# A weighted sum over eight experts: a ring of token slots in place of four load buffers, and three terms of the last tokens on TensorE

## The chip, the cores and the metric

The kernel runs on one core of a Trainium2 chip. The metric is device time in microseconds (us), the median of several executions. The profile and the trace come from one more execution, in which the hardware profiler recorded every instruction and every DMA packet.

## What is computed

For each of 16 x 1024 tokens there are eight expert outputs of 512 numbers and eight weights. The result is the weighted sum over the experts:

```python
batch, seq, n_experts, expert_dim = 16, 1024, 8, 512
weights = combine_weights[..., np.newaxis]
return np.sum(expert_outputs * weights, axis=2).astype(np.float32)
```

Everything is float32. The expert outputs are 268.4 MB, the result 33.6 MB, the weights 0.5 MB. Each expert output is used once, in one multiply and one add.

## The kernel before

The 16,384 tokens are cut into 64 steps of 128 partitions x 2 tokens (J = 2). A token of a partition is one row of 8 x 512 floats, 16 KB; a step's load is 4 MB, 32 KB for each partition, and one stretch of HBM. A "token" below means one such row in each of the 128 partitions, so there are 128 of them; one multiply-add over one expert of one token is a tile of 128 x 512.

Loads (issue_load, L52 to L62) go alternately through SP's and ScalarE's DMA queue, three steps ahead of their use (LA = 3), into four buffers (in_pool). Each step has its own small weight load through GpSimd's queue (L60). The last two steps (K_TAIL = 2) are loaded as two halves each, one token at a time (L59).

For each of the first 62 steps VectorE does all the arithmetic: for each token one multiply by the first weight (L77) and seven multiply-adds into the accumulator in place (L83), one token after the other. The result of a step, 4 KB per partition, is stored through the queue that did not load it (L92).

The last two steps are shared: ScalarE multiplies experts 4 to 7 into bf16 products (L111), VectorE does experts 0 to 3 (L116, L122), adds the products up in two halvings (L130, L135) and onto the accumulator (L138), and each token is stored by itself through SP's queue (L141).

The order on each engine is the order in the program as the tile framework schedules it; a DMA instruction waits in its issuing engine's queue until its buffer is free, and everything behind it on that engine waits too.

Of the kernel before, what the change touches and what calls it, by code (L numbers as in the profile page):

```python
# [1 line left out]

# [4 lines left out]


@with_exitstack  # L10
def kernel(
    ctx: ExitStack,
    tc: tile.TileContext,
    expert_outputs: bass.AP,
    combine_weights: bass.AP,
    out: bass.AP,
):
    nc = tc.nc
    fp32 = mybir.dt.float32
    bf16 = mybir.dt.bfloat16  # L20

    B, S, E, D = expert_outputs.shape
    T = B * S
    P = 128
    J = 2
    n_steps = T // (P * J)

    eo_blk = expert_outputs.rearrange("b s e d -> (b s) e d").rearrange(
        "(n p j) e d -> n p j e d", p=P, j=J
    )  # L30
    w_blk = combine_weights.rearrange("b s e -> (b s) e").rearrange(
        "(n p j) e -> n p j e", p=P, j=J
    )
    o_blk = out.rearrange("b s d -> (b s) d").rearrange(
        "(n p j) d -> n p j d", p=P, j=J
    )

    in_pool = ctx.enter_context(tc.tile_pool(name="in_pool", bufs=4))
    w_pool = ctx.enter_context(tc.tile_pool(name="w_pool", bufs=4))
    out_pool = ctx.enter_context(tc.tile_pool(name="out_pool", bufs=4))  # L40
    prod_pool = ctx.enter_context(tc.tile_pool(name="prod_pool", bufs=2))

    ES = E // 2
    K_TAIL = 2

    load_engines = [nc.sync, nc.scalar]

    LA = 3
    in_tiles: list[bass.AP | None] = [None] * n_steps
    w_tiles: list[bass.AP | None] = [None] * n_steps  # L50

    def issue_load(m: int) -> None:  # L52
        in_t = in_pool.tile([P, J, E, D], fp32, name="in_t")
        w_t = w_pool.tile([P, J, E], fp32, name="w_t")
        if m < n_steps - K_TAIL:
            load_engines[m % 2].dma_start(out=in_t, in_=eo_blk[m])
        else:
            for j in range(J):
                load_engines[m % 2].dma_start(out=in_t[:, j], in_=eo_blk[m, :, j])  # L59
        nc.gpsimd.dma_start(out=w_t, in_=w_blk[m])  # L60
        in_tiles[m] = in_t
        w_tiles[m] = w_t  # L62

    for m in range(min(LA, n_steps)):
        issue_load(m)

    for n in range(n_steps):
        if n + LA < n_steps:
            issue_load(n + LA)
        if n >= n_steps - K_TAIL:  # L70
            continue
        in_tile = in_tiles[n]
        w_tile = w_tiles[n]
        acc = out_pool.tile([P, J, D], fp32)

        for j in range(J):
            nc.vector.tensor_scalar_mul(  # L77
                out=acc[:, j, :],
                in0=in_tile[:, j, 0, :],
                scalar1=w_tile[:, j, 0:1],  # L80
            )
            for e in range(1, E):
                nc.vector.scalar_tensor_tensor(  # L83
                    out=acc[:, j, :],
                    in0=in_tile[:, j, e, :],
                    scalar=w_tile[:, j, e : e + 1],
                    in1=acc[:, j, :],
                    op0=mybir.AluOpType.mult,
                    op1=mybir.AluOpType.add,
                )  # L90

        load_engines[(n + 1) % 2].dma_start(out=o_blk[n], in_=acc)  # L92

    tail_steps = list(range(n_steps - K_TAIL, n_steps))
    tail_accs = {}
    tail_prods = {}
    for n in tail_steps:
        acc = out_pool.tile([P, J, D], fp32, name="acc")
        prods = prod_pool.tile([P, J, E - ES, D], bf16, name="prods")
        tail_accs[n] = acc  # L100
        tail_prods[n] = prods

    for j in range(J):
        for n in tail_steps:
            in_tile = in_tiles[n]
            w_tile = w_tiles[n]
            acc = tail_accs[n]
            prods = tail_prods[n]

            for e in range(ES, E):  # L110
                nc.scalar.mul(  # L111
                    out=prods[:, j, e - ES, :],
                    in_=in_tile[:, j, e, :],
                    mul=w_tile[:, j, e : e + 1],
                )
            nc.vector.tensor_scalar_mul(  # L116
                out=acc[:, j, :],
                in0=in_tile[:, j, 0, :],
                scalar1=w_tile[:, j, 0:1],
            )  # L120
            for e in range(1, ES):
                nc.vector.scalar_tensor_tensor(  # L122
                    out=acc[:, j, :],
                    in0=in_tile[:, j, e, :],
                    scalar=w_tile[:, j, e : e + 1],
                    in1=acc[:, j, :],
                    op0=mybir.AluOpType.mult,
                    op1=mybir.AluOpType.add,
                )
            nc.vector.tensor_add(  # L130
                out=prods[:, j, 0:2, :],
                in0=prods[:, j, 0:2, :],
                in1=prods[:, j, 2:4, :],
            )
            nc.vector.tensor_add(  # L135
                out=prods[:, j, 0, :], in0=prods[:, j, 0, :], in1=prods[:, j, 1, :]
            )
            nc.vector.tensor_add(  # L138
                out=acc[:, j, :], in0=acc[:, j, :], in1=prods[:, j, 0, :]
            )  # L140
            nc.sync.dma_start(out=o_blk[n, :, j], in_=acc[:, j, :])  # L141


# [1 line left out]
_INS = ['expert_outputs', 'combine_weights']  # L145
_OUTS = [((16, 1024, 512), 'float32')]


# [23 lines left out]
```

## Time and profile before

| | |
|---|---|
| median of 5 runs | 721.49 us (721.30 to 721.65) |
| the profiled execution | 721.57 us |
| its span (first to last instruction) | 719.8 us |
| VectorE busy | 644.3 us, 90% |
| ScalarE busy | 11.4 us, 2% |
| DMA moved | 302.63 MB, 420 GB/s over the span |
| busy multiply-adds (L83) | 580.1 us, 868 of 744 ns each |

The profile cuts the span into 40 equal slices of 18 us and gives for each the busy tenths of an engine, and for the DMA engines the busy tenths and the GB/s moved. A group line has the source line, the engine, the operation, its output and inputs, the shape, the count, and behind the bar the busy time in us, the mean duration in ns and the idle time just before. Two instructions of one engine can overlap a little, so a count times the mean can exceed the busy time. A packet is one row that a DMA engine copies; sixteen engines share the 128 partitions, so each copies eight of a load's 128 rows.

### The profile page before, as it was taken

What the parts mean: (1) busy time and instruction counts of PE and PEld (TensorE: products, weight loads), DVE (VectorE), ACT (ScalarE), POOL (GpSimd) and SP (SyncE); (2) the same over time, 40 slices, a digit from 0 to 9 for tenths busy, and PEclk for the clock granted to TensorE, in tenths of its full rate; (3) what the DMA queues carried; (4) which work ended last, traced back from release to release, by engine and by line L of the source; (5) the groups of instructions that cost most, each with busy time, mean ns of one, the idle gap of its engine ahead of it and who ended that gap; (6) DMA issues with size and microseconds to landing.
All of it is one profiled execution on the core that took longest, in us unless ns stands there. A gap on an engine that the chain in (4) does not pass through costs nothing.

```text
span 719.8 us, 1532 instructions
## 1 busy us (share of the span) xinstructions
DVE 644.3 (90%) x1020; ACT 11.4 (2%) x17; POOL 35.6 (5%) x68
## 2 busy tenths in 40 slices
DVE  0799999999998999989998999989998999999977
ACT  0000000000000000000000000000000000000023
POOL 1000000000000000000000000000000000000000
DMA  9999999999999999999999999999999999999983
GB/s 380 437 418 447 429 427 430 427 424 436 441 435 430 427 424 427 432 433 440 433 429 426 430 427 428 446 430 431 430 427 427 432 435 435 434 427 425 426 357 135
DMA packets 21068, 302.63 MB, mean 420 GB/s; under 512 B 3136, under 2 KB 4160, under 8 KB 12608
## 3 DMA queue, kind: packets, MB, share of 16 engines
q1 hardware_dynamic: 9792, 151.52, 49.2%
q10 hardware_dynamic: 9216, 150.47, 49.0%
q0 software_dynamic: 2048, 0.53, 0.3%
q14 instruction: 12, 0.10, 0.0%
HBM read 268.96 MB, written 33.55 MB: 420 GB/s over the span
## 4 chain that ended last, share of the span: by engine, by line
DMA 64%; DVE 35%; issue 1%; DVEq 0%; SPq 0%
DMA out_dram<-acc 56%; DVE acc L83 30%; DMA in_t<-in_expert_outputs_dram 8%; DVE acc L77 3%; DVE acc L122 1%; DVE acc L138 0%; DVE prods L130 0%; DVE acc L116 0%; DVE prods L135 0%; DVEq L77 0%; DVEq L116 0%; SPq L92 0%
## 5 line engine op out<-in xcount | busy, mean ns | idle before, releaser
L83 DVE SCALAR_TENSOR_TENSOR acc<-in_t,w_t,acc 128x512 f32<-128x512 f32 x868 | 580.1, 744 | 0.0
L77 DVE TENSOR_SCALAR acc<-in_t,w_t 128x512 f32<-128x512 f32 x124 | 54.6, 482 | 66.2 <-DMA in_t<-in_expert_outputs_dram 43.2
L60 POOL DMA_DIRECT2D w_t<-in_combine_weights_dram x64 | 35.4, 554 | 637.7 <-DVE acc L83 636.9
L111 ACT ACT_TABLE_LOAD x1 | 1.3, 1283 | 690.4 <-DMA in_t<-in_expert_outputs_dram 690.4
L111 ACT ACTIVATE prods<-in_t,w_t 128x512 bf16<-128x512 f32 x16 | 10.1, 708 | 9.4 <-DMA in_t<-in_expert_outputs_dram 9.4
L122 DVE SCALAR_TENSOR_TENSOR acc<-in_t,w_t,acc 128x512 f32<-128x512 f32 x12 | 8.8, 743 | 0.0
L116 DVE TENSOR_SCALAR acc<-in_t,w_t 128x512 f32<-128x512 f32 x4 | 1.9, 480 | 5.6 <-DMA out_dram<-acc 5.6
L138 DVE TENSOR_TENSOR acc<-acc,prods 128x512 f32<-128x512 f32 x4 | 2.7, 684 | 0.0
L130 DVE TENSOR_TENSOR prods<-prods 128x1024 bf16<-128x1024 bf16 x4 | 2.7, 682 | 0.0
L135 DVE TENSOR_TENSOR prods<-prods 128x512 bf16<-128x512 bf16 x4 | 1.7, 416 | 0.0
L156 POOL MEMSET const-float32-0.0<- 128x1 f32 x1 | 0.1, 99 | 0.2 <-issue 0.2
L156 POOL MEMSET const-bfloat16-1.0<- 128x1 bf16 x1 | 0.1, 101 | 0.0
L156 POOL MEMSET const-float32-1.0<- 128x1 f32 x1 | 0.1, 99 | 0.0
L156 POOL MEMSET const-uint8-127<- 128x1 uint8 x1 | 0.1, 99 | 0.0
## 6 DMA issues: line engine op xcount, KB each, us to landing
in_t<-in_expert_outputs_dram ACTq DMA_DIRECT2D x31, 4096.0 KB, 33.5
in_t<-in_expert_outputs_dram SPq DMA_DIRECT2D x31, 4096.0 KB, 33.3
out_dram<-acc ACTq DMA_DIRECT2D x31, 512.0 KB, 33.5
out_dram<-acc SPq DMA_DIRECT2D x31, 512.0 KB, 33.4
in_t<-in_expert_outputs_dram SPq DMA_DIRECT2D x2, 2048.0 KB, 31.2
in_t<-in_expert_outputs_dram ACTq DMA_DIRECT2D x2, 2048.0 KB, 14.2
w_t<-in_combine_weights_dram POOLq DMA_DIRECT2D x64, 8.0 KB, 6.8
out_dram<-acc SPq DMA_DIRECT2D x4, 256.0 KB, 2.6
```

Source lines behind the costliest of these rows:

```text
L60: nc.gpsimd.dma_start(out=w_t, in_=w_blk[m])
L77: nc.vector.tensor_scalar_mul(out=acc[:, j, :], in0=in_tile[:, j, 0, :], scalar1=w_tile[:, j, 0:1],)
L83: nc.vector.scalar_tensor_tensor(out=acc[:, j, :], in0=in_tile[:, j, e, :], scalar=w_tile[:, j, e : e + 1], in1=acc[:, j, :], op0=mybir.Al ...
L111: nc.scalar.mul(out=prods[:, j, e - ES, :], in_=in_tile[:, j, e, :], mul=w_tile[:, j, e : e + 1],)
L116: nc.vector.tensor_scalar_mul(out=acc[:, j, :], in0=in_tile[:, j, 0, :], scalar1=w_tile[:, j, 0:1],)
L122: nc.vector.scalar_tensor_tensor(out=acc[:, j, :], in0=in_tile[:, j, e, :], scalar=w_tile[:, j, e : e + 1], in1=acc[:, j, :], op0=mybir.Al ...
L130: nc.vector.tensor_add(out=prods[:, j, 0:2, :], in0=prods[:, j, 0:2, :], in1=prods[:, j, 2:4, :],)
L135: nc.vector.tensor_add(out=prods[:, j, 0, :], in0=prods[:, j, 0, :], in1=prods[:, j, 1, :])
L138: nc.vector.tensor_add(out=acc[:, j, :], in0=acc[:, j, :], in1=prods[:, j, 0, :])
L156: nc = _bacc.Bacc("TRN2", target_bir_lowering=False, num_devices=1)
```

## The change

One tile, the ring, has ten slots of one token (160 KB per partition) and takes the place of the four load buffers. Tokens are grouped by eight in each partition (G = 8), so that one partition's eight tokens are 128 KB of HBM in a row, and the next partition's eight follow. Loads fill up to four slots at once, 64 KB per partition, cut where the ring or a group of eight ends: 4, 4, 2, 4, 2, 4, 4, 4, 2, 2, 4, 4 tokens, and so on up to token 112; then two at a time; the last two tokens in halves and in pieces of 3, 2, 2 and 1 experts. All loads go through SP's queue.

All weights are loaded by one DMA at the start, ahead of the loads on the same queue. ScalarE makes the first term (weight times expert 0) of each token, two tokens ahead; VectorE adds the other seven, taking two tokens in turn, expert by expert. The accumulators are one tile of 16 tokens; eight tokens are stored by one DMA of 16 KB per partition through ScalarE's queue, and at the end four, two, one and one, the last three of them through SP's.

For the last eight tokens ScalarE makes a diagonal matrix of each of the first three weights (from an identity that GpSimd makes at the start), TensorE multiplies it with the expert's tile in fp32 and sums the three in PSUM, and VectorE adds the other five terms, the first of them onto the PSUM tile. `pin` keeps an instruction in program order.

```diff
-    J = 2
+    pin = tc.keep_in_program_order
+    G = 8
+    SLOTS = 10
+    PE_TOKENS = 8
+    PE_EXPERTS = 3
...
+    x = expert_outputs.rearrange("b s e d -> (b s) e d").rearrange(
+        "(n p g) e d -> n p g e d", p=P, g=G
+    )
+    w = combine_weights.rearrange("b s e -> (b s) e").rearrange(
+        "(n p g) e -> p n (g e)", p=P, g=G
+    )
...
+    ring = one.tile([P, SLOTS, E, D], fp32, name="ring")
+    acc = one.tile([P, 2 * G, D], fp32, name="acc")
+    w_t = one.tile([P, T_P, E], fp32, name="w_t")
+    ident = one.tile([P, P], fp32, name="ident")
+    loads = []
+    BULK = 112
+    t = 0
+    while t < BULK:
+        m = min(4, SLOTS - t % SLOTS, G - t % G)
+        loads += [(t, m, 0, E)]
+        t += m
+    for t in range(BULK, T_P - 2, 2):
+        loads += [(t, 2, 0, E)]
+    loads += [(T_P - 2, 1, 0, 4), (T_P - 2, 1, 4, 8)]
+    loads += [(T_P - 1, 1, 0, 3), (T_P - 1, 1, 3, 5), (T_P - 1, 1, 5, 7), (T_P - 1, 1, 7, 8)]
+    def load_until(t):
+        nonlocal loaded
+        while loaded < len(loads) and loads[loaded][0] + loads[loaded][1] <= t:
+            i, m, e0, e1 = loads[loaded]
+            n, g, s = i // G, i % G, i % SLOTS
...
+            pin(nc.sync.dma_start(out=dst, in_=src))
+            loaded += 1
+    def first(i):
+        s, a = i % SLOTS, i % (2 * G)
+        if i < T_P - PE_TOKENS:
+            pin(nc.scalar.mul(out=acc[:, a], in_=ring[:, s, 0], mul=w_t[:, i, 0:1]))
+            return
+        ps = ps_pool.tile([P, D], fp32, name="ps")
+        for e in range(PE_EXPERTS):
+            diag = diag_pool.tile([P, P], fp32, name="diag")
+            pin(nc.scalar.mul(out=diag, in_=ident, mul=w_t[:, i, e : e + 1]))
+            nc.tensor.matmul(
+                ps, lhsT=diag, rhs=ring[:, s, e], start=e == 0, stop=e == PE_EXPERTS - 1
+            )
+        sums[i] = ps
+    def term(i, e):
+        s, a = i % SLOTS, i % (2 * G)
+        if i < T_P - PE_TOKENS:
+            before, e0 = acc[:, a], 1
         else:
+            before, e0 = (sums[i] if e == PE_EXPERTS else acc[:, a]), PE_EXPERTS
+        if e >= e0:
+            pin(
+                nc.vector.scalar_tensor_tensor(
+                    out=acc[:, a],
+                    in0=ring[:, s, e],
+                    scalar=w_t[:, i, e : e + 1],
+                    in1=before,
+                    op0=mult,
+                    op1=add,
+                )
+            )
+    def store(i, m, queue):
+        n, g, a = i // G, i % G, i % (2 * G)
+        pin(queue.dma_start(out=o[n, :, g : g + m], in_=acc[:, a : a + m]))
...
+    pin(nc.sync.dma_start(out=w_t.rearrange("p (n g) e -> p n (g e)", g=G), in_=w))
+    make_identity(nc, ident)
+    load_until(SLOTS - 2)
+    for i in (0, 1):
+        first(i)
+    for i in range(0, T_P, 2):
+        load_until(i + SLOTS)
+        for k in (i + 2, i + 3):
+            if k < T_P:
+                first(k)
+        for e in range(E):
+            for k in (i, i + 1):
+                term(k, e)
+        end = i + 2
+        if end <= T_P - G and end % G == 0:
+            store(end - G, G, nc.scalar)
+        elif end == T_P - 4:
+            store(end - 4, 4, nc.scalar)
+        elif end == T_P - 2:
+            store(end - 2, 2, nc.sync)
+        elif end == T_P:
+            store(end - 2, 1, nc.sync)
+            store(end - 1, 1, nc.sync)
```

## The prediction

> **What bounds the kernel now.** I read the page first (slices, queues, costliest groups), then the windows of the start, the middle and the end, then the timeline of the last 30 us. The slices and the queue shares:
>
> ```profile
> DVE  0799999999998999989998999989998999999977
> DMA  9999999999999999999999999999999999999983
> GB/s 380 437 418 447 429 427 430 427 424 436 441 435 430 427 424 427 432 433 440 433 429 426 430 427 428 446 430 431 430 427 427 432 435 435 434 427 425 426 357 135
> q1 hardware_dynamic: 9792, 151.52, 49.2%
> q10 hardware_dynamic: 9216, 150.47, 49.0%
> ```
>
> The 16 DMA engines are full from the first slice to the 38th; both hardware queues together take 98.2% of their time. VectorE has gaps. So the middle is paid in bytes, and only the first and the last slices are paid in something else. The windows (us, VectorE, ScalarE and GpSimd busy, clock, DMA share, GB/s):
>
> ```profile
> 43.00:52.00 9.00, 9.00 (x16) 0.00 (x0) 0.62 (x1) 1.00 0.99 424
> 54.00:63.00 9.00, 9.00 (x14) 0.00 (x0) 0.06 (x1) 1.00 1.03 441
> 160.00:640.00 480.00, 440.55 (x694) 0.00 (x0) 23.50 (x44) 1.00 1.01 431
> 684.00:708.40 24.40, 18.26 (x31) 8.85 (x13) 0.00 (x0) 1.00 0.84 325
> 708.40:719.80 11.40, 7.76 (x14) 2.56 (x4) 0.00 (x0) 1.00 0.20 74
> ```
>
> Steady rate 431 GB/s. The last load packet ends at 708.4 us (packet records of the trace). In the 24.4 us before that the engines stand 16%, 3.9 us; behind it 11.4 us of arithmetic and last stores remain. The groups and the end of the timeline:
>
> ```profile
> L83 DVE SCALAR_TENSOR_TENSOR acc<-in_t,w_t,acc 128x512 f32<-128x512 f32 x868 | 580.1, 744 | 0.0
> L135 DVE TENSOR_TENSOR prods<-prods 128x512 bf16<-128x512 bf16 x4 | 1.7, 416 | 0.0
> 708.54 0.74 DVE L122 SCALAR_TENSOR_TENSOR acc<-in_t,w_t,acc 128x512 f32<-128x512 f32 x1
> 709.21 0.68 DVE L130 TENSOR_TENSOR prods<-prods 128x1024 bf16<-128x1024 bf16 x1
> 715.50 0.69 DVE L138 TENSOR_TENSOR acc<-acc,prods 128x512 f32<-128x512 f32 x1
> ```
>
> One multiply-add lasts 744 ns, but 580.1/868 = 0.668 us is what each occupies. The last VectorE instruction ends at 716.19, the span at 719.80: a last store costs 3.6 us. The profiled execution took 721.57 us, 1.77 more than its span; the median is 721.49. I sum against 721.57.
>
> **Part by part. VectorE in the middle.** The multiply by the first weight goes to ScalarE (120 times the 0.708 us of L111's multiplies: 85 us on an engine that has nothing else to do). VectorE keeps seven multiply-adds per token, 7 x 0.663 = 4.64 us, for 5.03. It is not the bound before, and is less so after: DMA moves 2.36 MB per token, 5.47 us at 431. Two chains in turn bring nothing: the bf16 L130 at 709.21, which doesn't read what L122 at 708.54 writes, starts 0.67 us behind it, as dependent L83s do. Priced at zero, and hidden if it weren't.
>
> **One load queue.** All loads go through SP, stores through ScalarE's queue. In 43:52 and 54:63 the packet records show loads on one queue alone (88% of the time, the rest stores of the other): 424 and 441 GB/s, mean 432. One queue fills the engines. Cost zero.
>
> **Ring.** A load of m tokens waits for m slots. When four tokens land, VectorE frees two after 0.7 + 14 x 0.663 = 10.0 us and four after 19.3; issue to first packet took 1.2 us in this trace (0.74 to 1.98). The least that can then be in flight is one four-token load (19.3 us of DMA), and the load behind it needs only two more slots: 11.2 us. With all six other slots in flight there are 29 us against 20.5. So 8 us of cover; if it were gone, a stall would come at some of the 12 loads per 40 tokens. ScalarE's stores stand in its queue behind the first multiplies of the next two tokens, and so behind their load: up to about 12 us late (a four-token load with its stores lasts 21.9, a pair 9.3); the accumulators last 16 tokens (87 us) and are rewritten only when token +16 lands. No cost.
>
> **Packets.** Records: a 2 KB packet takes 86 ns, 4 KB 159, 16 KB 611, 32 KB 1,213. Per engine the stores are 62 x 8 packets of 4 KB now, 78.9 us; as 15.5 x 8 packets of 16 KB they are 75.8 us: 3.1 us saved. Loads of 64 KB: no row; on the line of 16 and 32 KB they save at most 1 us more, which I leave out. The rate bound from the other side is the first rival.
>
> **Weights first.** One DMA of 2,048 rows of 256 B, 128 per engine, ahead of all loads. Nearest rows: the 512 B weight packets of now, 27 ns, and semaphore writes, 9 ns: 1.2 to 3.5 us, against the 2.3 us (0.3% of the span) that the small loads take now inside the stream. I take 1 us more, ends -1 and +1.5. First VectorE work shifts by some 2 us, covered: ten tokens are 48 us of DMA, the first four are free at about 44.
>
> **End of the load stream, X.** Bytes before it: 302.6 less the last four tokens' stores, about 301.5 MB, at 431: 699.5 us. Plus 2.0 to the first packet, 0.6 for the first packets (1.7 to 2.0 us for 1.2), less 3.1, plus 1.0: X = 700.0, against 708.4. The 3.9 us of standing engines go: the last six loads are all issued about eight tokens (39 us of loads) ahead. Bounds 698.5 and 703.1 (no saving on packets).
>
> **Tail.** Eight last tokens get terms 0 to 2 on TensorE, VectorE adds five (5 x 0.663). At 0.6 us per expert row: tokens 124/125 land at X - 9.8, the first half of 126 at X - 7.3, the first piece of 127 at X - 2.9, the last at X + 0.3. VectorE takes 124 and 125 in turn, so its second instruction waits for six matmuls: with m per fp32 matmul that pair ends at X - 9.8 + 6m + 9 x 0.663, and the last pair needs 10 x 0.663 = 6.6 more, or nine behind 127's sum, at best X - 9.8 + 12m. No matmul is in the trace. Below, the cheapest row over 512 columns, 0.416 (L135): VectorE ends at X + 5.3. Above, two fp32 passes of L83, 1.5: sums are late, X - 9.8 + 18 + 6.0 = X + 14.2. I take 1.0, between the ends, nearer to one fp32 pass with a weight load ahead of it: X - 9.8 + 6 + 6.0 + 6.6 = X + 8.8, and 0.5 for two hops between engines (the last load packet of now ends at 708.38, the multiply waiting for it starts at 708.66): X + 9.3. The six diagonals per pair on ScalarE need only the weights, and go ahead of the loads. Identity on GpSimd, early: zero.
>
> The Trainium skill's page "TensorE: Matmul & The Clock Gate", section Part 1, has the array stream one column per cycle, at 1.2 GHz until about 3.4 us of activity and at 2.4 after; it has no fp32 price. By it a single pass would be an estimated 0.43 us cold, and the time about that of the lower end, 711.2; were it four passes (my guess), 1.7 cold and 0.85 warm, some 722.5 and 713.8. No run shows it yet.
>
> Sum: 700.0 + 9.3 + 3.6 + 1.8 = **714.7 us**, 6.9 less: 8.4 from the earlier end of the loads, less 1.5 because what follows (12.9) is longer than now (11.4). The new tail is no gain by itself.
>
> **Rivals.** (1) Cheap matmuls (0.42): 700.0 + 5.8 + 3.6 + 1.8 = 711.2. For it: nothing but the lowest row. (2) Slow matmuls (1.5): 700.0 + 14.7 + 3.6 + 1.8 = 720.1; twelve matmuls count, so it is slower than before by over 0.2% from 1.73 us each. For it: TensorE works in bursts with pauses, and only the last pair counts. (3) Slower than before: long rows lower the load rate. A load now reads whole 4 MB stretches; after, rows of at most 64 KB at a pitch of 128 KB. For it: no row has that pitch. Against it: L59's 16 KB rows at 32 KB pitch take 611 ns, on the same line as contiguous 32 KB. The price at 424, the lower single-queue window: 301.5/424 is 711.1, X = 711.1 + 2.6 - 3.1 + 1.0 = 711.6, and the time 711.6 + 14.7 = 726.3. It decides where 301.5 MB take over 707.7 us, below 426 GB/s. (4) The packets bring nothing: X = 703.1, 717.8. (5) "Two chains" does nothing, by the rows above; that is already in the forecast.
>
> A rule of the Trainium skill speaks for rival 3: the page "DMA: Bandwidth & Descriptors", section "Latency and other measured facts", warns of power-of-two row pitches in HBM, with 207 GB/s at 512 KiB, 164 at 2 MiB, and 214 where a large pitch is padded. A pitch of 128 KiB lies below its list; by it an estimate of the worst is 207/214, 3% or some 23 us (738), and by its trend nothing. The trace's 1,213 ns decides only for the 32 KB pitch.
>
> **Chances.** Forecast 0.57, cheap matmuls 0.13, slow matmuls 0.15 (a third each faster, within, slower), slow rate 0.09 (0.07 slower, 0.02 within), packets for nothing 0.06. 0.2% is 1.4 us, about what a measurement of this kernel can tell from no change. Faster: 0.57 + 0.13 + 0.06 + 0.05 = 0.81; within: 0.05 + 0.02 = 0.07; slower: 0.05 + 0.07 = 0.12. The range runs from the cheap matmuls to the slow ones, 711.0 to 720.6: about 0.05 is left out below, 0.15 above.
>
> **What would show it.** Right: GB/s at 430 to 434 up to the 38th slice; VectorE multiply-adds still 0.66 apart, its share near 80%, waiting for loads; store packets of 16 KB; last load packet near 700; about 9 us from there to the last multiply-add. Wrong: GB/s at 425 or less in the middle (rival 3), DMA slices under 9 before the 39th (ring), a matmul group whose mean is 1.5 us or more, or VectorE's wait for TensorE ending last (rival 2).

## The result: 719.83 us, 0.19% faster where 0.94% was forecast

The changed kernel takes 719.83 us (median of 26 runs, 719.3 to 721.24), the kernel before beside it 721.40 (46 runs). The ratio is 0.9981, 95% interval 0.9975 to 0.9986: 1.4 us, just clear of what can be told from no change. The direction was right and the time lies in the range given, near its upper end, but the gain is less than a quarter of the 6.9 us forecast. The profiled execution took 719.75 us with a span of 717.8, so the parts below are compared with 721.57 and 719.8.

The page of the changed kernel: slices, queues, the three costliest groups and TensorE's.

```profile
DVE  0499888799697969897789877879897799997657
PEclk9999999999999999999999999999999999999978
DMA  9999999999999999999999999999999999999992
GB/s 365 420 447 426 427 438 420 449 410 448 435 425 448 427 423 441 427 449 420 446 413 460 420 435 435 431 422 444 419 454 430 435 417 435 429 433 433 428 409 89
q1 hardware_dynamic: 9264, 270.01, 87.4%
q10 hardware_dynamic: 2304, 32.51, 10.6%
q14 instruction: 9, 0.07, 0.0%
L111 DVE SCALAR_TENSOR_TENSOR acc<-ring,w_t,acc 128x512 f32<-128x512 f32 x872 | 580.1, 745 | 112.3 <-ACT acc L92 112.3
L92 ACT ACTIVATE acc<-ring,w_t 128x512 f32<-128x512 f32 x120 | 77.7, 711 | 556.4 <-DMA ring<-in_expert_outputs_dram 556.4
L98 PE MATMUL ps<-ring,diag 128*128 128x512 f32 x48 | 27.6, 739 | 679.6 <-DMA ring<-in_expert_outputs_dram 679.6
```

The DMA engines are now full one slice longer, the 39th, which held 357 GB/s before and holds 409. VectorE stands more, 112.3 us, nearly always for ScalarE's first term, which stands for loads (556.4 us). TensorE appears in the last three slices only, 24 matmuls as 48 instructions, and there the clock falls. The line of q14 is the one that I read past in the page before, where it had 12 packets: instructions being fetched, in the profile's list of what the same 16 DMA engines carry.

The windows (us, busy time of TensorE, its weight loads, VectorE, ScalarE, GpSimd, then clock, DMA share, GB/s), and below them the chain that ended last:

```profile
160.00:640.00 480.00, 0.00 (x0) 0.00 (x0) 413.09 (x622) 56.96 (x88) 0.00 (x0) 1.00 1.00 433
690.00:695.00 5.00, 1.25 (x4) 0.32 (x3) 3.82 (x6) 0.00 (x0) 0.00 (x0) 1.00 1.00 414
695.00:700.00 5.00, 5.00 (x8) 2.07 (x9) 2.78 (x5) 1.86 (x6) 0.00 (x0) 0.66 0.97 392
700.00:705.00 5.00, 5.00 (x13) 2.26 (x12) 3.17 (x6) 0.00 (x0) 0.00 (x0) 1.00 0.23 94
```

```profile
660.87 34.02 DMA ring<-in_expert_outputs_dram
694.90 7.10 PE ps L98 x12
702.02 4.79 DVE acc L111 x8
```

433 GB/s in the middle for 431 is 0.46%, of 700 us some 3.2 us, about the 3.1 us of the packets; that one rate doesn't tell the larger stores from the larger loads or from the missing small weight loads. Then, from 700 us on, the share is 0.23 although a load has still not landed. The chain says which wait counts: the load of tokens 124 and 125 lands at 694.9, six matmuls end at 702.0, and from there VectorE works almost without a gap to 714.7. My sum had that load at 690.2.

The landings of that one load, each of its 16 DMA engines reporting by itself, follow. (Landing times here and below are from the trace's records and count from a zero some 0.2 us ahead of the profile's; that touches no difference between two landings.) They are: the first at 687.1, the 8th at 688.8, the 15th at 690.0, the 16th at 694.9. The last load's are 697.7, 698.8, 700.0 and 707.2. One engine of the 16 is late, and a load has landed when the latest has.

How late, over the run: the 16th landing minus the 8th, in us, for the loads and stores of the kernel before that land in each stretch (the small weight loads left out), and when packets of the instruction queue ran:

```
before, us      43-54  61-131  143-209  220-297  309-374  386-463  475-541  552-629  641-685
16th minus 8th   0.2    0.9      1.8      2.5      3.3      4.2      4.9      5.7      6.5
8 KB instruction packets at: 57  137  214  302  (323  346)  379  (434)  468  546  634
after, most loads: 1.6 at 153-196, 2.6 at 309-328, 3.6 at 372-416, 4.5 at 460-528, 5.1 at 616-626, 6.1 at 661-671, 8.4 at the last
8 KB instruction packets at: 71  158  251  (279)  356  444  540  (587)  633
```

In the kernel before the lag rises in steps, and each step is at one instruction packet. The spacing, 77 to 89 us, is that of 112 to 130 VectorE instructions (16 to a step of 10.97 us); the packets in brackets, in between, make no step. In the changed kernel the 15th landing too is 1.5 us behind the 8th from the first load on, and the packets at 71 and 158 show no step; those at 251, 356, 444, 540 and 633 do. The lag is 6.1 at tokens 124 and 125. The rise to 8.4 behind that is at no instruction packet: there the late engine has the store of tokens 120 to 123 among its last loads, eight packets of 8 KB at 0.31 us, 2.5 us. That the late engine is the same one all along is inferred from a lag that is never made good; the records don't name it.

So from here the theories. **A:** each block of VectorE's instructions costs one DMA engine 0.6 to 0.9 us, nobody takes over its equal share of every load, and the end waits for that engine. **B:** the end is bound by the arithmetic behind the loads (cold TensorE, the order of the multiply-adds), or the engine is slow by itself.

### The profile page after: what moved, and what is told of

It reads as the page before. It is cut to its first block, busy times and chain, and to the rows that moved or that the text cites. A ratio compares the mean times of both kernels' runs of the same rounds, so it can differ in the third digit from the quotient of the medians.

```text
span 717.8 us, 1363 instructions
## 1 busy us (share of the span) xinstructions
PE 27.6 (4%) x48; PEld 11.2 (2%) x48; DVE 585.5 (82%) x880; ACT 86.7 (12%) x145; POOL 0.7 (0%) x6
## 4 chain that ended last, share of the span: by engine, by line
DMA 63%; DVE 33%; ACT 1%; issue 1%; PE 1%; SPq 0%; DVEq 0%; ACTq 0%
DMA ring<-in_expert_outputs_dram 63%; DVE acc L111 33%; ACT acc L92 1%; PE ps L98 1%; ACT L92 0%; DVEq L173 0%; SPq L83 0%; SPq L125 0%; ACTq L92 0%; DVEq L111 0%
## 5 line engine op out<-in xcount | busy, mean ns | idle before, releaser
L111 DVE SCALAR_TENSOR_TENSOR acc<-ring,w_t,acc 128x512 f32<-128x512 f32 x872 | 580.1, 745 | 112.3 <-ACT acc L92 112.3
L92 ACT ACTIVATE acc<-ring,w_t 128x512 f32<-128x512 f32 x120 | 77.7, 711 | 556.4 <-DMA ring<-in_expert_outputs_dram 556.4
L98 PE MATMUL ps<-ring,diag 128*128 128x512 f32 x48 | 27.6, 739 | 679.6 <-DMA ring<-in_expert_outputs_dram 679.6
L98 PEld LDWEIGHTS ps<-ring,diag 128*128 128x128 f32 x48 | 11.2, 240 | 695.1 <-issue 693.7
L111 DVE SCALAR_TENSOR_TENSOR acc<-ring,w_t,ps 128x512 f32<-128x512 f32 x8 | 5.9, 746 | 16.9 <-PE ps L98 16.9
L97 ACT ACTIVATE diag<-ident,w_t 128x128 f32<-128x128 f32 x24 | 7.9, 390 | 29.7 <-DVE acc L111 26.7
```

The source lines that it names most:

```text
L92: pin(nc.scalar.mul(out=acc[:, a], in_=ring[:, s, 0], mul=w_t[:, i, 0:1]))
L97: pin(nc.scalar.mul(out=diag, in_=ident, mul=w_t[:, i, e : e + 1]))
L98: nc.tensor.matmul(ps, lhsT=diag, rhs=ring[:, s, e], start=e == 0, stop=e == PE_EXPERTS - 1)
L111: nc.vector.scalar_tensor_tensor(out=acc[:, a], in0=ring[:, s, e], scalar=w_t[:, i, e : e + 1], in1=before, op0=mult, op1=add,)
```

## Experiments

Ratios are to the kernel before, run beside each on the same chip; the changed kernel's is 0.9981.

**A probe for the late engine.** Loads cut by partitions, so that fewer engines share them.

```diff
+    cuts = {56: [(0, 120), (120, 128)], 70: [(0, 126), (126, 128)], 80: [(0, 104), (104, 128)],
+            94: [(0, 88), (88, 128)], 104: [(0, 119), (119, 128)]}
-            pin(nc.sync.dma_start(out=dst, in_=src))
+            for p0, p1 in cuts.get(i, [(0, P)]):
+                pin(nc.sync.dma_start(out=dst[p0:p1], in_=src[p0:p1]))
```

> A probe, not a version. In the changed kernel 15 of the 16 DMA engines land a load together and one comes 5 to 8 us later by the end (load of tokens 124 and 125: 8th landing 688.8, last 694.9). Five loads are cut by partitions into two DMAs each, so that the first of them is shared by fewer engines: tokens 56 to 59 as 120 + 8 partitions (15 + 8 engines), 70 and 71 as 126 + 2 (14 + 2), 80 to 83 as 104 + 24 (13 + 12), 94 and 95 as 88 + 40 (11 + 10), 104 to 107 as 119 + 9 (7 + 9). If the low-numbered engines are the ones used, the load after which the lag of the last landing falls from 3-5 us to under 1 names the late engine: 15, 14, 13, 11 or 12, 9 to 7. Theory A (one engine is late because it also fetches VectorE's instructions): the lag grows by steps of 0.6 to 0.9 us about every 80 us until it is relieved, then starts again from nothing. Rival (every engine is late at times): no cut ends the lag. Time is not the question; 719 to 730 us.

It took 918.76 us (one run) and named no engine. Its windows:

```profile
160.00:300.00 140.00, 0.00 (x0) 0.00 (x0) 118.37 (x179) 16.79 (x26) 0.00 (x0) 1.00 1.00 433
300.00:400.00 100.00, 0.00 (x0) 0.00 (x0) 51.85 (x79) 6.45 (x10) 0.00 (x0) 1.00 1.00 280
```

Up to the first cut load all is as before; then the rate falls to 280 GB/s with the engines busy all the time, and it never recovers (311 from 400 to 600 us, 276 from 600 to 900). 64 KB packets take 3,005 ns on average for 2,428. The landings of one load spread over tens of us, so no lag can be read. Why one uneven load slows those behind it was not pursued. A miss, and a warning: the late engine can't be relieved this way.

**More VectorE instructions.**

```diff
+    idle = one.tile([P, 1], fp32, name="idle")
+    for r in range(256):
+        nc.vector.memset(idle, 0.0)
```

> 256 writes of one column by VectorE are added at the start, where it waits 26 us for the first load. Nothing else changes. Theory A (each 8 KB block of VectorE's instructions that is fetched costs one DMA engine 0.6 to 0.9 us, and no other engine takes over its share): two blocks of 128 instructions more, the last landing of the load of tokens 124 and 125 comes 1.2 to 1.8 us later than 694.9 and the time is 721.0 to 721.6. Rival (the late engine is slow by itself, about 1%): lag and time as they are, 719.8.

722.95 us (721.72 to 723.58), ratio 1.0020 (1.0011 to 1.0029). The load of 124 and 125 lands at 697.2 for 694.9, and the lag at the last load is 10.5 for 8.4. That is the direction of A, and above its size. But the 256 writes took 31.9 us, longer than VectorE's idle time, so it began its first multiply-add at 32.8 instead of 28.7, and the ring ran dry for a moment (164 GB/s from 56 to 58 us). The lag stepped up only behind that. Not clean; the next one is.

**GpSimd instructions instead.** The same tile, 1,024 writes by GpSimd, VectorE untouched.

> GpSimd, which has nothing else to do, writes one column 1,024 times at the start; VectorE is left alone. Theory A (each 8 KB block of an engine's instructions costs one DMA engine 0.6 to 0.9 us): eight blocks are fetched in the first 110 us, and after that the last landing of a load comes 5 to 7 us behind the middle one, where it is 1.6 us behind in the changed kernel. If these blocks go through the DMA engine that fetches VectorE's, the lag at the end is 13 to 15 us for 8.4 and the time 724 to 726; if through another, 719.5 to 721. Rival (the lag has nothing to do with instructions): 1.6 us at 110, 719.8.

720.29 us (719.55 to 721.56), ratio 0.9983 (0.9974 to 0.9991). Its instruction queue:

```profile
q14 instruction: 17, 0.14, 0.0%
```

Eight blocks more than the changed kernel's nine, at 12 to 152 us. The lag behind the middle engine is 5.0 at 156 us, where the changed kernel has 1.6; then it stays flat (4.8 to 5.0 at most loads) up to 592 us, while VectorE's blocks go on, and ends at 8.2 like the changed kernel's 8.4. So instructions make a DMA engine late, even those of an engine that does nothing useful: 0.4 us a block here counted from a lag of 1.6, 0.6 counted from nothing. And GpSimd's go through another DMA engine than VectorE's: the two lags don't add, and the second late engine can be seen coming up from behind, as the 15th landing lies 2.0 behind the 8th at 330 us, 3.0 after VectorE's block at 358, 4.0 after the one at 446 and 4.8 after the one at 539. It costs nothing, because the other engine is later still at the end. That the lag had nothing to do with instructions is excluded.

**Fewer VectorE instructions.** Experts 1 to 4 left out for the first 112 tokens, all loads and the whole tail kept.

```diff
-        if e >= e0:
+        if e >= e0 and not (i < T_P - 16 and e in (1, 2, 3, 4)):
```

> Leaves out experts 1 to 4 of tokens 0 to 111 on VectorE (their loads, the first terms, the stores and the whole tail stay), so VectorE has 432 multiply-adds for 880, and three to four 8 KB blocks of instructions fewer to fetch. Theory A (each block costs one DMA engine 0.6 to 0.9 us that it never gets back): the lag of the last landing behind the middle one at the last load is 4 to 6 us for 8.4, tokens 124/125 land at 692 to 693 for 694.9, and the time is 716.8 to 717.8. Rival (one engine is slower by itself, or the lag comes with bytes): lag and time as they are, 719.3 to 720.2.

717.42 us (716.79 to 717.94), ratio 0.9944 (0.9931 to 0.9956): 2.4 us faster by the medians.

```profile
q14 instruction: 6, 0.05, 0.0%
160.00:640.00 480.00, 0.00 (x0) 0.00 (x0) 183.14 (x274) 56.93 (x88) 0.00 (x0) 1.00 1.00 433
```

Three blocks less. The rate in the middle is the same 433 GB/s with less than half the work on VectorE, so VectorE is no bound there; the middle engine lands tokens 124 and 125 at 688.3 (688.8 before the edit), the late one at 692.2 (694.9). Of these 2.7 us, 0.5 are common to all engines; the lag itself falls from 6.1 to 3.9, 0.7 us a block. A holds, by adding and by taking away.

**Stores behind the last loads.** If the end waits for the late engine's loads, the stores of tokens 112 to 123, 7.3 us of DMA, need not stand among them.

```diff
-            store(end - G, G, nc.scalar)
+            store(end - G, G, nc.scalar if end < T_P - G else nc.sync)
         elif end == T_P - 4:
-            store(end - 4, 4, nc.scalar)
+            store(end - 4, 4, nc.sync)
```

> The last 2 MB store (tokens 112 to 119) and the 1 MB store (120 to 123) go through SP's queue, behind all loads, instead of through ScalarE's queue beside them. Theory A (the end hangs on when the late engine lands tokens 124 to 127): 4.9 us of store leave the stream ahead of token 125 and 2.4 more ahead of 127, so 124/125 land at 690 for 694.9, the last piece at 700 for 707.2, the last multiply-add ends 5 us earlier, 709.8 for 714.7, and the time is 714.5 to 716. The stores that are left, 16 tokens, take 9.8 us behind the loads and are hidden up to about 711. Rival (the end is bound by arithmetic or by all bytes together, whatever their order): 719.0 to 719.8.

714.10 us (712.29 to 716.04), ratio 0.9890 (0.9870 to 0.9910). The timeline:

```profile
689.43 12.23 PE L98 MATMUL ps<-ring,diag 128*128 128x512 f32 x24 [2.70 <-DMA ring<-in_expert_outputs_dram]
703.83 5.38 DVE L111 SCALAR_TENSOR_TENSOR acc<-ring,w_t,acc 128x512 f32<-128x512 f32 x8
```

Tokens 124 and 125 land 5.4 us earlier (689.5 for 694.9), the last piece at 699.5 for 707.2, the last multiply-add ends at 709.2 for 714.7. The arithmetic behind the landing is unchanged, and all of the shift reaches the end. The middle engine's landing moves by about as much as the late one's (5.2 us), and the lag at the last load is 5.8 for 8.4. So this run shows that the end hangs on the landings, whatever makes one engine late. It gives 5.7 us more than the change, which was forecast to give 6.9 in all.

**Without TensorE.** PE_TOKENS = 0: ScalarE makes the first term of the last eight tokens too, VectorE adds seven.

> The last eight tokens are done as all others: ScalarE the first term, VectorE seven; TensorE does nothing. Theory A (the end is set by when the late engine lands tokens 124 to 127): pair 124/125 ends at 694.9 + 0.7 + 14 x 0.663 = 704.9, the last pair waits for the last token's first piece (705.4) and takes 14 x 0.663 = 9.3: 715.4 for 714.7, time 720.0 to 721.0. Rival (TensorE's three terms take 6 multiply-adds of the last pair off the end, 4.0 us): 723.8.

718.77 us (718.59 to 719.36), ratio 0.9963 (0.9951 to 0.9976): faster by 1.1 us than with TensorE, and faster than I expected, because VectorE did not have to wait for the last token: it starts at 695.2, 0.6 us behind the landing, and runs 28 multiply-adds to 713.8. With TensorE it does 20, but starts at 699.5 and can go on only at 702.0. Together with the late stores:

> Late stores, and the last eight tokens by ScalarE and VectorE alone. 124/125 land at 689.5, then 0.7 and 28 multiply-adds 0.663 apart end at 708.9, the span at 712.0 and the time 713.5 to 714.5, the same as with TensorE (714.1): TensorE with a cold clock is worth nothing in either version. Rival (once the stores are out of the way arithmetic binds, and TensorE takes 6 multiply-adds off): 716 to 718.

714.51 us (713.64 to 715.52), ratio 0.9909 (0.9893 to 0.9924), against 714.10 with TensorE: no difference, as expected. Three terms by TensorE as the change has them are worth nothing.

**A warm TensorE.**

```diff
+        if i in (T_P - 7, T_P - 5):
+            for r in range(12):
+                pin(nc.tensor.matmul(hot, lhsT=ident, rhs=ident, start=True, stop=True))
```

> Twelve matmuls of the identity by itself, whose result nobody reads, are put behind the sums of tokens 121 and 123, so that TensorE doesn't stand for 5 us before the next pair. If the granted clock is what made the sums of 124 and 125 take 7.1 us (0.66 of the clock at 695 to 700), they take 5.2 to 5.6, and the end comes 1.5 to 1.9 us earlier: 717.9 to 718.4. Rival (the sums wait for their diagonals or for landings, not for the clock): no change, 719.3 to 719.9.

719.90 us (718.35 to 723.33), ratio 0.9981 (0.9968 to 0.9994): no change. But the clock was not kept:

```profile
690.00:695.00 5.00, 1.39 (x14) 1.23 (x12) 4.79 (x8) 0.00 (x0) 0.00 (x0) 1.00 1.00 415
695.00:700.00 5.00, 5.00 (x8) 2.19 (x9) 0.46 (x1) 1.86 (x6) 0.00 (x0) 0.66 1.03 418
```

The added matmuls ended at 691.4 and the next load landed at 695.0. The pause of 3.6 us was enough: 0.66 of the clock again. The experiment therefore didn't test what it was made for; in the last one below the clock is kept, but together with two other edits.

**One token after the other.**

```diff
-        for e in range(E):
-            for k in (i, i + 1):
+        for k in (i, i + 1):
+            for e in range(E):
                 term(k, e)
```

> VectorE finishes one token before it begins the next, all along. My reading: in the middle nothing changes (multiply-adds 0.66 apart, dependent or not). At the end token 124 starts when its own sum is ready (699.4) instead of waiting for 125's, and 126 is done before 127: 125 from 702.9 to 706.2, 126 to 709.5, 127 to 712.8 for 714.7, so 1.5 to 2.8 us faster, 717.0 to 718.3. Rival (taking turns hides a latency of the accumulator): multiply-adds in the middle over 0.68 us apart; the time the same or longer, 719.8 or more.

718.36 us (717.95 to 719.83), ratio 0.9958 (0.9945 to 0.9970): 1.5 us less than the changed kernel, as expected, but not for the reason expected. The end:

```profile
692.56 13.47 PE L98 MATMUL ps<-ring,diag 128*128 128x512 f32 x24 [4.63 <-DMA ring<-in_expert_outputs_dram]
710.27 3.11 DVE L111 SCALAR_TENSOR_TENSOR acc<-ring,w_t,acc 128x512 f32<-128x512 f32 x4
```

TensorE has tokens 124 and 125 at 692.6 for 694.9, 2.3 us earlier. From there it is 5.5 us to the first multiply-add on a sum (4.6 in the changed kernel; TensorE stayed cold longer) and 15.3 us more to the end (15.2): the order brought nothing. What came earlier is the landing. VectorE, slower now, lets the store of tokens 112 to 119 start only at 680.0 for 670.8, and the middle engine has tokens 124 and 125 down 5.6 us earlier. So far as the trace shows, it is the effect of the late stores, by accident.

The reading of the middle was wrong too. The group and the window of 200 to 600 us, first of this kernel, then the window of the changed one:

```profile
L111 DVE SCALAR_TENSOR_TENSOR acc<-ring,w_t,acc 128x512 f32<-128x512 f32 x872 | 645.6, 751 | 59.6 <-ACT acc L92 32.9
200.00:600.00 400.00, 0.00 (x0) 0.00 (x0) 379.18 (x514) 48.20 (x74) 0.00 (x0) 1.00 1.00 433
```

```profile
200.00:600.00 400.00, 0.00 (x0) 0.00 (x0) 339.52 (x512) 46.39 (x72) 0.00 (x0) 1.00 1.00 433
```

The same number of multiply-adds keeps VectorE busy 379 us of 400 instead of 340. One that reads what the one ahead of it wrote starts 0.787 us behind it (starts at 300.96 and 301.75, for example), not 0.663. Taking turns does hide something, 0.12 us each; only there is enough room in the middle that the 433 GB/s stay.

**Packet sizes.** Loads of at most two tokens:

```diff
-        m = min(4, SLOTS - t % SLOTS, G - t % G)
+        m = min(2, SLOTS - t % SLOTS, G - t % G)
```

> Loads of at most two tokens, 32 KB per partition, in place of four. By the packet records a 64 KB packet takes 2,418 ns and two of 32 KB take 2,426: 11 packets fewer per engine and 8 ns each make 1.4 us of DMA time; the extra loads also wait for slots two at a time, so more is in flight. Packets count: 0.5 to 1.5 us slower, 720.3 to 721.3. Rival (smaller loads keep the engines closer together, since they take turns with stores in smaller pieces): 0.5 to 1.5 us faster, 718.3 to 719.3.

And stores of two tokens up to token 120:

```diff
-        if end <= T_P - G and end % G == 0:
-            store(end - G, G, nc.scalar)
+        if end <= T_P - G:
+            store(end - 2, 2, nc.scalar)
```

> Up to token 120 every pair is stored by itself, 4 KB per partition, as in the kernel before, through ScalarE's queue; the last eight tokens as they are. My term of 3.1 us for larger store packets says 2.9 us slower (15 eighths of 16 KB at 611 ns become 4 KB at 159): 722.3 to 723, and 431 GB/s in the middle for 433. Rival (the gaps between packets, not their size, carry that overhead, and it is hidden): 719.5 to 720.5.

721.72 us (721.00 to 722.49), ratio 1.0004 (0.9995 to 1.0013) for the loads, 722.75 (719.86 to 724.43), ratio 1.0016 (1.0007 to 1.0026) for the stores. The middle of each, in that order:

```profile
160.00:640.00 480.00, 0.00 (x0) 0.00 (x0) 408.93 (x612) 57.36 (x86) 0.00 (x0) 1.00 1.00 432
```

```profile
160.00:640.00 480.00, 0.00 (x0) 0.00 (x0) 407.29 (x613) 57.39 (x88) 0.00 (x0) 1.00 1.00 428
```

Small loads cost 1.9 us by the medians, of which the packets are 1.4 (176 more for each engine, 8 ns each); the lag at the last load is 9.3 for 8.4. Small stores cost 2.9 us by the medians, near the predicted term, but that agreement is partly luck. The rate fell further than I said (428, not 431), and in the profiled execution the middle engine lands tokens 124 and 125 some 6.6 us later, while the lag of the late one there is 3.7 for 6.1. Why many small stores leave the loads' lag smaller was not pursued. Each size by itself is worth at least what the whole change has gained.

**All of it together.** Late stores; the warm TensorE; and for the last four tokens turns in which each token starts as its sum is ready.

```diff
+        turns = [(k, e) for e in range(E) for k in (i, i + 1)]
+        if i == T_P - 4:
+            turns = [(i + int(a), int(e)) for a, e in (
+                "03 04 05 13 06 14 07 15 23 16 24 17 25 33 26 34 27 35 36 37".split())]
+        elif i == T_P - 2:
+            turns = []
+        for k, e in turns:
+            term(k, e)
```

> Late stores and warm TensorE together, and for the last four tokens an order of multiply-adds in which each token starts as its sum is ready (124 alone, then 124 and 125 in turn, 125 and 126, 126 and 127). 124/125 land at 690.0, the sums are there at 692.7, 695.3, 697.9 and 700.5, twenty multiply-adds end at 706 to 707. By arithmetic the end would be 710 and the time 711.8; but the late engine still has its loads and all stores to do, 709.6 at the earliest by the changed kernel's records, plus 1.5 to the end of the span and 1.8: 712.9. I expect 712.5 to 714. Rival (the sum of the two single gains): 713.5 to 715.

712.59 us (712.18 to 713.13), ratio 0.9874 (0.9861 to 0.9888): 8.9 us faster than the kernel before.

```profile
690.00:696.00 6.00, 5.75 (x14) 2.67 (x15) 5.42 (x9) 0.00 (x0) 0.00 (x0) 1.00 1.05 431
696.00:702.00 6.00, 4.79 (x12) 1.81 (x10) 6.00 (x10) 0.00 (x0) 0.00 (x0) 1.00 0.70 296
```

Here the pause ahead of the last pairs is 0.8 us and the clock stays at 1.00; the six matmuls of 124 and 125 end 5.4 us after they start, for 7.1. The last multiply-add ends at 707.3. The two small last stores land at 709.5 and 710.1, and the span ends at 710.9. The expectation had the late engine's bytes as the bound; they are one by half a microsecond only, since the 15 other engines have the last store down at 709.5. What the clock and the order bring one by one was not measured, and against late stores alone (714.10, two of its five runs at 712.3 and 712.5) so few runs don't settle a gain.

## Why the prediction was right in direction and wrong in size

**The end of the load stream, X: the step that failed.** It was put at 700.0 from bytes and a mean rate. It has no term for engines that land apart. The middle engine of the 16 landed the last load at 698.8 and the 15th at 700.0, so the sum came out right for 15 engines. The 16th landed it at 707.2: 6.1 us of its 8.4 us behind the middle engine were there at tokens 124 and 125, and the rest came with the store of tokens 120 to 123, since with that store moved the lag stays 5.8 to the end. In the kernel before I took the 3.9 us of standing engines from 684 to 708.4 for a gap in the supply of loads that the ring would close ("the 3.9 us of standing engines go"). They don't: in the changed kernel the DMA share from 683 to 707.2 us is 0.73, and the engines stand 6.5 us of it. In the kernel before, too, 15 engines were waiting for one that was 6.5 us behind. ScalarE's last two loads were issued only when the load ahead of them had landed:

```profile
690.43 1.28 ACT L111 ACT_TABLE_LOAD   x1 [690.43 <-DMA in_t<-in_expert_outputs_dram]
690.58 0.82 ACTq L59 DMA_DIRECT2D in_t<-in_expert_outputs_dram  x2
```

15 engines had landed that load by 684.5, the last one at 690.4. The change took this wait away, but not the late engine: nine blocks of instructions are fetched for twelve, but VectorE's, which make the late engine late, are hardly fewer (880 instructions for 1,020).

The sum from the profiled execution, term by term: landing of 124 and 125 4.7 us later than predicted (694.9 for 690.2); the arithmetic behind it 0.7 longer (19.8 for 19.1); end of the span 0.5 shorter (3.1 for 3.6); outside the span 0.15 more. Together 5.05, from 714.7 to 719.75.

**Packets: near in size, in part by luck.** 3.1 us predicted, 433 GB/s for 431, and 2.9 us when undone, by two shifts against each other (see the small stores). The 64 KB loads, left out as at most 1 us, are worth 1.9; by the prediction's own rows, some 8 ns for each of 176 packets saved, it should have been 1.4.

**One queue, ring, weights: right.** No DMA slice is below 9 before the last; a window of 480 us on one load queue holds 433. The 256 B packets took 18 ns, 128 per engine 2.3 us, inside the bounds. The cover of the ring was thinner than I said at one place: VectorE began at 28.7 us, and 4 us more emptied the ring. I had put the first VectorE work some 2 us later than before; it began 5.9 later (28.7 for 22.9). The last load was issued 17 us ahead and not 39, which was still early enough.

**VectorE in the middle: the conclusion right, the reason wrong.** I held L83 rows 0.663 apart for dependent neighbours. The scheduler of the kernel before had taken two tokens in turn already, as its rows "L77 x2, L83 x14" could have told, and as the 0.663 itself says once the dependent distance is known to be 0.787; so the change removed no wait there.

**TensorE: the size close, by luck.** 1.0 us a matmul assumed, 7.10/6 = 1.18 measured, as a mean of cold and warm ones that the sum did not have. The second rival's time, 720.1, is nearly the one measured, but for another reason: at 1.18 us a matmul its own arithmetic gives 716. "The new tail is no gain by itself" held: without TensorE the kernel is 1.1 us faster. One of the two instructions of a matmul was issued every 0.43 us warm and 0.85 us cold, so a single pass was not the price, and my guess of four was: about 0.86 and 1.7 us a matmul. A pause of 3.6 us let the clock fall (0.66) and one of 0.8 us did not (1.00); but with late stores one of 2.70 us was enough:

```profile
690.00:695.00 5.00, 5.00 (x9) 2.02 (x8) 3.56 (x6) 0.00 (x0) 0.00 (x0) 0.66 1.07 437
```

The Trainium skill's page "TensorE: Matmul & The Clock Gate", Part 1, has the clock fall after an idle window of about 3.4 us. These runs show it after less.

**Slower load rate at a 128 KB pitch: excluded.** 433 GB/s. The Trainium skill's page "DMA: Bandwidth & Descriptors", section "Latency and other measured facts", warns of power-of-two pitches from 512 KiB up; at 128 KB, below its list, the pitch costs nothing here.

## What to carry to other kernels

Where transfers are spread evenly over the DMA engines and nothing rebalances them, the end waits for the latest engine and not for the mean rate: read the 16 landings of a late load one by one, not the GB/s. Here every 8 KB of VectorE's instructions delayed one engine for good, and its 880 instructions were a cost at the end though VectorE was idle nearly a fifth of the time; 1,024 of GpSimd's, on another DMA engine, cost nothing, because that engine was not the latest. And ask of each transfer in the last stretch whether something waits for it: stores that nobody waits for belong behind the loads that somebody waits for.

## What the runs showed of the hardware that was not expected

A block of 8 KB of instructions, whose packet is recorded at 0.31 us, costs its DMA engine 0.4 to 0.9 us (steps of 0.7 to 0.9 in the kernel before, 0.7 a block by taking three away, 0.4 to 0.6 for GpSimd's). VectorE's and GpSimd's blocks pass through different DMA engines; which, the records don't say, and why a block costs more than its packet is open.

The Trainium skill's page "DMA: Bandwidth & Descriptors", section "Latency and other measured facts", calls two engines of the 16 usually slower and guesses at the descriptor rings of GpSimd's DMAs. The changed kernel issues no DMA from GpSimd, and its one late engine is late in steps that follow the instructions.

A few loads cut unevenly over the partitions brought the rate from 433 GB/s down to 276 to 311 for the rest of the kernel. That cause is open too.
